# A hybrid mLSTM / GLA / sparse-attention block: x in its own pool, background work in smaller portions, high parts first

## The chip, the cores and the metric

The kernel runs on one core of a Trainium2 chip. The metric is the time of one execution in device microseconds (us): the median of three runs of the kernel before is 1209.51 us (1208.49 to 1209.81). The profile is of one more execution.

## What is computed

Two layers (`DEPTH = 2`) work on x, 512 rows by 1024 columns in float32. Each layer normalises x, multiplies it by a wide weight matrix (9312 columns), runs three mixers on the pieces, and multiplies the gated results back to 1024 columns:

```python
p = split_columns(rmsnorm(x, norm_g) @ w_in)
...
hm = mlstm_chunkwise(heads(mq, ML_HEADS), heads(mk, ML_HEADS), heads(p['ml_v'], ML_HEADS), li, lf).astype(dt)
...
hg = gla_chunked(heads(p['gla_q'], GLA_HEADS), heads(p['gla_k'], GLA_HEADS),
                 heads(p['gla_v'], GLA_HEADS), heads(la, GLA_HEADS)).astype(dt)
...
hd = dsa_sparse_attention(dq, dk, heads(p['dsa_v'], DSA_HEADS), iq, p['idx_k'], iw, rel_bias, topk)
...
y = jnp.concatenate([y_ml, y_gla, y_dsa], axis=-1) @ w_out
return x + y
```

The sparse attention picks 128 keys for each query by an index score; the kernel finds them with 16 rounds of "eight largest, then strike them out".

## The kernel before

**Three passes for a product.** A float32 product is made of three fast passes. Each operand is split in a high part (a copy in the type `F32R`, on ACT) and a low part (the rest, on DVE). `mm3` issues high times high, high times low and low times high into one PSUM sum. The high and low parts of the normalised, transposed x are `xhi` and `xlo`, 8 slices of 128 rows by 512 columns each. Weights arrive in pieces of 128 x 1024 (`raw`), which `prepare()` turns into `hi` (ACT) and `lo` (DVE), one piece ahead of the need. `need(p)` makes sure that both parts of a piece are issued.

**The three kinds of projection.** `wide` has x as the stationary operand and the weights moving (PSUM tile `pn`, 512 columns); a unit has four pieces and four blocks `sb` of 128 rows, and a block takes 24 matmuls, 6 of each piece. `proj_t` has the weights stationary and x moving (`pt`, 512 columns, or 384 for the index queries). `w_out_part` has the gated results `yhi`, `ylo` stationary and the weights moving (`pw`, 512 columns). Twelve `wide` units stand in a layer. All matmul, copy and DMA calls go through one recorder, so that nearly all rows of the trace have the line L178; the tiles' names tell the place.

**Background work.** Everything else (the mLSTM products `psS` and `pom`, GLA's `psga`, `psst`, `pog`, the index scores `pss`, the attention `psl`, `pst`, `pod`, the transposes `psx`, `psy`, `psq`) is written as generators. After every few projection matmuls the program calls `tick()`, which lets `Background` run steps of those tasks that a clock model says are ready. The model is only a planner: it runs while the program is built and sets the order in which instructions are issued; on the chip each engine goes through its queue in that order and waits on semaphores. `TICK_PE = 1.3` is how much TensorE time, in the model's us, the steps of one tick may add before it ends; `PRIORITY` sorts the ready tasks, low numbers first (`"scores": 0`, `"gla": 2`, `"sel": 4`). The model books 512 columns of a projection at 512/2210 + 0.002 = 0.2337 us (`Meter.cost`).

**Where tiles lie.** SBUF pools lie one behind the other in each partition in the order of their creation: `const`, `par`, `wp`, `wk`. Tiles with tags of their own follow each other in the order of first use, sizes rounded up to 32 bytes. `xhi` and `xlo` (16384 bytes a partition each) and `qz0`, `qz1` (2048 each) stand at the end of `const`, with `lev` (256) behind them; then `par` has two `pv` (448 each) and `zw` (1024). Then come the 12 weight tiles of `wp` (4096 each, tag `w`), and right behind them in `wk` the ten tiles with tag `t4` (4096 each), among them `yhi`, `ylo` and mLSTM's `ml_q`, `ml_k`. From the start of `xhi` to that of the first weight tile it is 2 x 16384 + 2 x 2048 + 256 + 2 x 448 + 1024 = 39040 bytes, which is 76 x 512 + 128. All slices of x, of the weights and of `t4` tiles that matmuls take begin at multiples of 512 bytes from their tile's start.

The leading block of a `wide` unit goes through the same path as the others, piece by piece:

```python
for j in range(2):
    k = 2 * i + j
    mm3(pss[sb], xhi[:, k, s], xlo[:, k, s], wh[j], wl[j], k == 0, k == KT - 1)
```

Of the kernel before, what the change touches and what calls it, by code (L numbers as in the profile page):

```python
# [10 lines left out]
F32 = mybir.dt.float32  # L11
F32R = mybir.dt.float32r
# [8 lines left out]
S = 512  # L21
D = 1024
DEPTH = 2
NB = S // 128
KT = D // 128
# [104 lines left out]


PAR_W = 108
TICK_PE = 1.3
TICK_K, TICK_T = 4, 2
SEMAPHORE, PIPE = 0.2, 0.13
BEHIND = {"sel": ("dve",)}
BACKLOG = {None: 11.0, "sel": 0.3}
ALONE = ("gla", "ml", "sel", "scores")
BUFFERS = {"gla": 6, "dsa": 4, "ml": 4, "mlv": 1, "conv": 2, "qk": 2, "y": 2, "scores": 4, "gates": 5}
PRIORITY = {"conv": 1, "y": -1, "norm": 0, "split": 0, "ml": 0, "mlv": 2, "scores": 0, "gla": 2, "dsa": 2, "sel": 4}  # L140


def pack_parameters(p):
# [131 lines left out]
class Background:  # L275
# [41 lines left out]
    def pick(self):  # L317
        for task in sorted(self.tasks, key=lambda t: PRIORITY.get(t["kind"], 1)):
            if self.startable(task) and self.due(task) <= self.clock.at["pe"]:
                return task  # L320

    def tick(self):
        end = self.clock.at["pe"] + TICK_PE
        task = self.pick()
        while task and self.clock.at["pe"] < end:
            self.step(task)
            task = self.pick()
# [14 lines left out]
def hybrid_kernel(ctx, tc, a, out, dbg=None):  # L342
    bass_nc = tc.nc
    clock = Clock()
# [14 lines left out]
    W_BUFS, RAWS, LOAD = 12, 2, 4.5  # L359
    const = ctx.enter_context(tc.tile_pool(name="const", bufs=1))  # L360
    par = ctx.enter_context(tc.tile_pool(name="par", bufs=2))
    wp = ctx.enter_context(tc.tile_pool(name="wp", bufs=2))
    wk = ctx.enter_context(tc.tile_pool(name="wk", bufs=2))
    sm = ctx.enter_context(tc.tile_pool(name="sm", bufs=8))
# [4 lines left out]
    def pp(name):  # L369
        t = psp.tile([128, 512], F32, tag="pp", name=name)  # L370
        clock.ring("pp", t, 3)
        return t
# [37 lines left out]
        nc.vector.memset(head[r, odd:odd + 1], 1.0)  # L410
    pad = const.tile([128, 8], F32, name="pad")
    nc.vector.memset(pad, 0.0)
    xhi = const.tile([128, KT, S], F32R, name="xhi")
    xlo = const.tile([128, KT, S], F32R, name="xlo")
    qzs = [const.tile([128, 2, 64 * NB], F32, name=f"qz{i}") for i in range(2)]
    for t in qzs:
        for odd, r in enumerate(HALVES):
            nc.gpsimd.memset(t[r, 1 - odd], 0.0)
# [45 lines left out]
    to_split, half_done, held, wanted = [], [], [], []  # L464
    state = {"used": 0, "raw": 0, "unit": 0}

    def w_tile(name, dtype):
        return wp.tile([128, 1024], dtype, tag="w", name=name, bufs=W_BUFS)

    def make_room(most=RAWS):  # L470
        while to_load and state["raw"] < most:
            if state["used"] + 1 > W_BUFS - (2 if any(p.hi is None for p in wanted) or not held else 0):
                break
            p = to_load.pop(0)
            state["used"] += 1
            state["raw"] += 1
            p.raw = w_tile("raw", F32)
            nc.sync.dma_start(p.raw, a["w_pack"][p.layer, p.at])
            p.loaded = clock.at["pe"] + LOAD
            to_split.append(p)  # L480

    def prepare():
        if half_done:
            p = half_done.pop()
            lo = w_tile("lo", F32R)
            nc.vector.tensor_sub(lo, p.raw, p.hi.bitcast(F32))
            state["used"] -= 1
            state["raw"] -= 1
            p.parts = [[t[:, c:c + p.n] for c in range(0, 1024, p.n)] for t in (p.hi, lo)]
            make_room()  # L490
        if to_split and to_split[0].loaded <= clock.at["pe"] and state["used"] + 2 <= W_BUFS:
            p = to_split.pop(0)
            state["used"] += 2
            p.hi = w_tile("hi", F32R)
            nc.scalar.activation(p.hi, p.raw, AF.Copy)
            half_done.append(p)

    def need(p):
        while p.parts is None:
            if not half_done:  # L500
                clock.at["pe"] = max(clock.at["pe"], to_split[0].loaded)
            prepare()
        return p.parts

    def take(kind, at=None):
        spec, pieces = units[state["unit"]]
        assert spec[0] == kind and (at is None or spec[1] == at), (spec, kind, at)
        state["unit"] += 1
        wanted.extend(pieces)
        held.extend(pieces)  # L510
        return pieces


    def give_back():
        p = held.pop(0)
        wanted.remove(p)
        state["used"] -= 2
        make_room()
# [3 lines left out]
    def tick():  # L522
        prepare()
        bg.tick()

    def mm3(ps, lh, ll, rh, rl, first, last):
        nc.tensor.matmul(ps, lhsT=lh, rhs=rh, start=first, stop=False)
        nc.tensor.matmul(ps, lhsT=lh, rhs=rl, start=False, stop=False)
        nc.tensor.matmul(ps, lhsT=ll, rhs=rh, start=False, stop=last)


    def proj_t(pieces, blk, s0=0, last=False):
        ps = pp("pt")
        c = slice(128 * blk, 128 * blk + 128)
        for k in range(KT):
            n = KT // len(pieces)
            wh, wl = need(pieces[k // n])
            mm3(ps[:, s0:S], wh[k % n][:, c], wl[k % n][:, c], xhi[:, k, s0:S], xlo[:, k, s0:S], k == 0, k == KT - 1)
            if last and k % n == n - 1:
                give_back()  # L540
            if k % TICK_T == TICK_T - 1 and k < KT - 1:
                tick()
        return ps
# [3 lines left out]
    def wide(pieces, f, before=None):  # L547
        pss = {}

        def part(sb, i):  # L550
            if i == 0:
                if before:
                    before(sb)
                pss[sb] = pp("pn")
            s = slice(128 * sb, 128 * sb + 128)
            wh, wl = need(pieces[i])
# [3 lines that stand above are left out]
            if sb == NB - 1:  # L560
                give_back()
            if i == 3:
                f(sb, pss.pop(sb))
            tick()

        lone = NB if before else NB - 2
        for sb in range(lone):
            for i in range(4):
                part(sb, i)
        if not before:  # L570
            for i in range(4):
                for sb in range(lone, NB):
                    part(sb, i)
# [104 lines left out]
    for layer in range(DEPTH):  # L678
# [45 lines left out]
        def y_group(name, hns, g0=0):  # L724
            yt, tasks = [], []

            def part(sb, ps):
                tasks.append(bg.start(y_part(yt, hns, ps, sb), "y"))
            wide(take("wide", OFF[name] + 256 * g0), part)
            return yt, tasks  # L730

        def w_out_part(q, yt, tasks, after=None):
            pieces = take("out", 512 * q)

            pss = {}
# [465 lines left out]
        zw = par.tile([80, 256], F32R, name="zw", bufs=1)  # L1201
        t_zw = bg.add(rank_weights())
        wide(take("wide", OFF["gla_v"]), keep_gv, lambda sb: bg.drain(norms[sb]))
        norms.clear()
        if layer == 0:
# [3 lines left out]
        ps = proj_t(w, 0, 0, True)  # L1209
# [47 lines left out]
        def dsa_qk_unit(g):  # L1257
            dst = [blocks(t4("dqk"), 2) for _ in range(2)]
            t_qk = []

            def part(sb, ps):
                t_qk.append(bg.start(qk_part(dst, ps, sb), "qk"))
            wide(take("wide", OFF["dsa_q"] + 256 * g), part)
            qks.append((dst, t_qk))
            if vs:
                dsa_tasks(g)
# [67 lines left out]
        for n, step in enumerate(PLAN):  # L1334
# [3 lines left out]
            _, name, g0, quarter = step  # L1338
# [32 lines left out]
```

## Time and profile before

| | |
|---|---|
| median of three runs | 1209.51 us (1208.49 to 1209.81) |
| the profiled execution | 1210.23 us, its span 1208.5 us |
| TensorE: matmuls busy | 1190.5 us, 99% of the span, 6004 of them |
| VectorE (DVE) busy | 832.7 us, 69% |
| ScalarE (ACT) busy | 600.4 us, 50% |
| GpSimd (POOL) busy | 169.6 us, 14% |
| DMA | 107.70 MB, mean 89 GB/s |
| granted TensorE clock, mean | 0.999 |

A page of the profile gives each engine's busy time, the idle time with what ended it, and the chain of work that ended last. PE is TensorE's matmuls, PEld its weight loads. Matmuls overlap in their pipeline, so the duration of one says little: what a matmul costs is the distance to the start of the next, which the chain's pieces show (so many matmuls in so many us).

### The profile page before, as it was taken

The numbers are of one execution on the slowest core, as the hardware profiler recorded it, in microseconds if no ns is written. First come the engines' busy times: TensorE is split into PE (matmuls) and PEld (weight loads), VectorE is DVE, ScalarE is ACT, GpSimd is POOL, SyncE is SP. The second block draws the span as 40 slices with busy tenths as digits, with TensorE's granted clock in tenths as the row PEclk, the third lists the DMA queues.
The fourth block names the chain that finished last, engine by engine and source line by source line (L and its number), as shares of the span: only waits on it lengthen the run. The fifth ranks groups of instructions, "written<-read, shape, count | busy, mean of one in ns | idle before, by whom it ended". The sixth has DMA issues, their size and how long they took to land.

```text
span 1208.5 us, 16501 instructions
## 1 busy us (share of the span) xinstructions
PE 1190.5 (99%) x6004; PEld 970.7 (80%) x6004; DVE 832.7 (69%) x1651; ACT 600.4 (50%) x1334; POOL 169.6 (14%) x309
## 2 busy tenths in 40 slices
PE   6999999999999999999999999999999999999998
PEld 4877788888888887888888778888888888887887
DVE  5577887977777766365566888878777778554643
ACT  6565546554353354762366654564453443646421
POOL 2101212320100011120010023041210010123000
PEclk9999999999999999999999999999999999999999
DMA  5333121221322233132224222222222223233221
GB/s 198 109 99 106 62 88 62 88 80 53 105 97 70 77 116 131 63 106 85 70 71 140 65 75 93 82 71 79 71 71 87 96 71 105 71 105 123 70 86 71
DMA packets 35152, 107.70 MB, mean 89 GB/s; under 512 B 5028, under 2 KB 8388, under 8 KB 35072
## 3 DMA queue, kind: packets, MB, share of 16 engines
q1 hardware_dynamic: 33136, 104.89, 26.7%
q0 software_dynamic: 1200, 1.36, 0.3%
q8 instruction: 47, 0.77, 0.3%
q10 hardware_dynamic: 736, 0.41, 0.1%
q14 instruction: 33, 0.27, 0.1%
HBM read 104.48 MB, written 3.43 MB: 89 GB/s over the span
## 4 chain that ended last, share of the span: by engine, by line
PE 88%; DVE 1%; issue 0%; ACT 0%; ACTq 0%
PE pn L178 42%; PE pt L178 17%; PE pw L178 14%; PE psS L178 3%; PE pom L178 2%; PE psga L178 1%; PE pod L178 1%; PE psl L178 1%; PE pog L178 1%; PE psy L178 1%; PE pst L178 1%; PE pss L178 1%; PE psq L178 1%; PE psx L178 0%; PE psst L178 0%; PE psd L178 0%
## 5 line engine op out<-in xcount | busy, mean ns | idle before, releaser
L178 DVE TENSOR_TENSOR lo<-raw,hi 128x1024 fp32r<-128x1024 f32 x178 | 219.4, 1233 | 141.1 <-ACT hi L178 134.5
L178 PE MATMUL pn<-hi,xhi 128*128 128x512 f32 x768 | 312.9, 407 | 0.0
L178 PE MATMUL pn<-lo,xhi 128*128 128x512 f32 x768 | 303.8, 396 | 0.6 <-DVE lo L178 0.6
L178 PE MATMUL pn<-hi,xlo 128*128 128x512 f32 x768 | 304.0, 396 | 0.0
L178 ACT ACTIVATE hi<-raw 128x1024 fp32r<-128x1024 f32 x178 | 188.7, 1060 | 202.4 <-PE pn L178 90.3
L178 PEld LDWEIGHTS pn<-hi,xlo 128*128 128x128 f32 x768 | 144.8, 189 | 35.2 <-DVE xlo L178 1.2
L178 PEld LDWEIGHTS pn<-lo,xhi 128*128 128x128 f32 x768 | 145.2, 189 | 32.2 <-DVE lo L178 1.2
L178 PEld LDWEIGHTS pn<-hi,xhi 128*128 128x128 f32 x768 | 145.2, 189 | 31.9 <-issue 0.8
L178 PE MATMUL pt<-xhi,hi 128*128 128x512 f32 (+1 forms) x400 | 158.7, 397 | 0.0
L178 PE MATMUL pt<-xhi,lo 128*128 128x512 f32 (+1 forms) x400 | 154.3, 386 | 0.0
L178 PE MATMUL pt<-xlo,hi 128*128 128x512 f32 (+1 forms) x400 | 154.2, 385 | 0.0
L178 PE MATMUL pw<-hi,yhi 128*128 128x512 f32 x256 | 101.7, 397 | 0.0
L178 PE MATMUL pw<-hi,ylo 128*128 128x512 f32 x256 | 99.9, 390 | 0.0
L178 PE MATMUL pw<-lo,yhi 128*128 128x512 f32 x256 | 99.7, 390 | 0.0
L178 PEld LDWEIGHTS pt<-xhi,hi 128*128 128x128 f32 x400 | 75.2, 188 | 17.6 <-issue 3.8
L178 PEld LDWEIGHTS pt<-xhi,lo 128*128 128x128 f32 x400 | 75.2, 188 | 14.9
L178 DVE TENSOR_TENSOR xr<-pw,xr 128x512 f32<-128x512 f32 x64 | 44.1, 689 | 60.6 <-PE pw L178 60.5
L178 PEld LDWEIGHTS pt<-xlo,hi 128*128 128x128 f32 x400 | 75.3, 188 | 12.6
L178 DVE SCALAR_TENSOR_TENSOR cacc<-cbuf,pv,cacc 128x512 f32<-128x512 f32 x96 | 73.3, 764 | 2.5 <-ACT el L178 0.2
L178 PEld LDWEIGHTS pw<-hi,ylo 128*128 128x128 f32 x256 | 48.0, 188 | 10.2
L178 PEld LDWEIGHTS pw<-lo,yhi 128*128 128x128 f32 x256 | 48.1, 188 | 9.3
L178 PEld LDWEIGHTS pw<-hi,yhi 128*128 128x128 f32 x256 | 48.1, 188 | 9.3
(188 smaller groups left out, 1661.3 us busy)
## 6 DMA issues: line engine op xcount, KB each, us to landing
raw<-w_pack SPq DMA_DIRECT2D x178, 512.0 KB, 3.5
xr<-x SPq DMA_DIRECT2D x4, 512.0 KB, 7.6
negm<-negm SPq DMA_DIRECT2D x8, 256.0 KB, 3.7
bs<-skew SPq DMA_DIRECT2D x8, 256.0 KB, 4.0
out_dram<-xr SPq DMA_DIRECT2D x8, 256.0 KB, 2.0
bs<-skew SPq DMA_DIRECT2D x8, 192.0 KB, 4.4
skew<-flat POOLq DMA_DIRECT2D x1, 1280.0 KB, 15.9
bs<-skew SPq DMA_DIRECT2D x8, 128.0 KB, 4.6
```

The lines of the kernel that those rows point to most:

```text
L178: return f(*args, **kw)
```

## The change

Three things are edited. `xhi`, `xlo`, `qz0` and `qz1` move from `const` to a pool `xt`, made between `par` and `wp`. From the start of `xhi` to the first weight tile it is now 2 x 16384 + 2 x 2048 = 36864 bytes, which is 72 x 512. `TICK_PE` goes from 1.3 to 0.7, and the priority of `scores` from 0 to 3, behind `gla`. And the leading block of each `wide` unit gets a function of its own, `first()`: for all four pieces the two passes that need only `hi`, then for all four the pass that needs `lo`; it ticks after each piece of the first half and after every other piece of the second.

```diff
-TICK_PE = 1.3
+TICK_PE = 0.7
...
-PRIORITY = {"conv": 1, "y": -1, "norm": 0, "split": 0, "ml": 0, "mlv": 2, "scores": 0, "gla": 2, "dsa": 2, "sel": 4}
+PRIORITY = {"conv": 1, "y": -1, "norm": 0, "split": 0, "ml": 0, "mlv": 2, "scores": 3, "gla": 2, "dsa": 2, "sel": 4}
...
+    xt = ctx.enter_context(tc.tile_pool(name="xt", bufs=1))
...
-    xhi = const.tile([128, KT, S], F32R, name="xhi")
-    xlo = const.tile([128, KT, S], F32R, name="xlo")
-    qzs = [const.tile([128, 2, 64 * NB], F32, name=f"qz{i}") for i in range(2)]
+    xhi = xt.tile([128, KT, S], F32R, name="xhi")
+    xlo = xt.tile([128, KT, S], F32R, name="xlo")
+    qzs = [xt.tile([128, 2, 64 * NB], F32, name=f"qz{i}") for i in range(2)]
...
+    def need_high(p):
+        while p.hi is None:
+            if not half_done:
+                clock.at["pe"] = max(clock.at["pe"], to_split[0].loaded)
+            prepare()
+        return [p.hi[:, c:c + p.n] for c in range(0, 1024, p.n)]
...
+        def first():
+            if before:
+                before(0)
+            ps = pp("pn")
+            s = slice(0, 128)
+            for i in range(4):
+                wh = need_high(pieces[i])
+                for j in range(2):
+                    k = 2 * i + j
+                    nc.tensor.matmul(ps, lhsT=xhi[:, k, s], rhs=wh[j], start=k == 0, stop=False)
+                    nc.tensor.matmul(ps, lhsT=xlo[:, k, s], rhs=wh[j], start=False, stop=False)
+                tick()
+            for i in range(4):
+                wl = need(pieces[i])[1]
+                for j in range(2):
+                    k = 2 * i + j
+                    nc.tensor.matmul(ps, lhsT=xhi[:, k, s], rhs=wl[j], start=False, stop=k == KT - 1)
+                if i % 2 == 0:
+                    tick()
+            f(0, ps)
+            tick()
...
         lone = NB if before else NB - 2
-        for sb in range(lone):
+        first()
+        for sb in range(1, lone):
             for i in range(4):
                 part(sb, i)
```

The order of issue shows three places. The first is PE in the first layer's first `wide` unit, right at the start (`psx` are transposes of x, `pn` the projection; numbers tell buffers apart, `hi_165` and `lo_190` are the parts of the fourth piece). The end of the leading block before:

```order
L178 MATMUL pn_183<-lo_190,xhi_100 128x512
L178 MATMUL pn_183<-hi_165,xlo_101 128x512
L178 MATMUL psx_237<-ident_82,xs_176 128x128 x4
L178 MATMUL psx_246<-ident_82,xs_176 128x128 x4
L178 MATMUL psx_260<-ident_82,xs_208 128x128 x4
L178 MATMUL pn_273<-hi_128,xhi_100 128x512
```

Now (the fourth piece is `hi_168`, `lo_191`):

```order
L178 MATMUL pn_186<-hi_168,xhi_103 128x512
L178 MATMUL pn_186<-hi_168,xlo_104 128x512
L178 MATMUL pn_186<-lo_134,xhi_103 128x512 x2
L178 MATMUL pn_186<-lo_147,xhi_103 128x512 x2
L178 MATMUL pn_186<-lo_164,xhi_103 128x512 x2
L178 MATMUL pn_186<-lo_191,xhi_103 128x512 x2
L178 MATMUL psx_238<-ident_85,xs_179 128x128 x4
L178 MATMUL psx_247<-ident_85,xs_179 128x128 x4
L178 MATMUL pn_266<-hi_131,xhi_103 128x512
```

The eight products with `lo` stand behind the sixteen with `hi`; and behind them 8 transposes where 12 stood, since block 2's (`xs_208`) moved back.

The second place is ACT at the same time: `zw` belongs to GLA's weights, `gv` empties the projection's PSUM tile, `xs` scales x for the transposes of blocks 1 to 3, `xhi` empties these.

```order
 L178 ACTIVATE zw<-wa 16x256 x2
+L178 ACTIVATE xs<-xr,rx 128x1024
 L178 ACTIVATE gv<-pn 128x256 x2
-L178 ACTIVATE xs<-xr,rx 128x1024 x2
-L178 ACTIVATE xhi<-psx,pv 128x128 x8
 L178 ACTIVATE xs<-xr,rx 128x1024
 L178 ACTIVATE xhi<-psx,pv 128x128 x16
-L178 ACTIVATE gv<-pn 128x256 x4
+L178 ACTIVATE xs<-xr,rx 128x1024
```

Block 1's `xs` is now ahead of `gv`, and block 2's `xs` behind it.

The third place is PE in the first mLSTM unit, where GLA's products (`psga`) and mLSTM's (`psS`) stand between the projection's matmuls. Before:

```order
L178 MATMUL psS<-ml_q,ml_k 128x384 x6
L178 MATMUL psga<-qz_102,dec 64x2x32 x8
L178 MATMUL pn<-hi,xhi 128x512
L178 MATMUL pn<-lo,xhi 128x512
L178 MATMUL pn<-hi,xlo 128x512
```

Now, behind the same `psS` row and three more `pn` rows like the first three of these:

```order
L178 MATMUL pn<-hi,xhi 128x512
L178 MATMUL pn<-lo,xhi 128x512
L178 MATMUL pn<-hi,xlo 128x512
L178 MATMUL psga<-qz_105,dec 64x2x32 x8
L178 MATMUL pn<-hi,xhi 128x512
```

What one tick issued together is now spread over two, with six projection matmuls between. Over the whole program the order has 4080 projection matmuls in both kernels; background work cuts them into 201 stretches before and 221 now. Of the 3312 matmuls of 512 columns that have x as an operand (`pn`, `pt`), the order now has 526 in stretches of up to 6, 560 in stretches of 8 to 12, 560 in stretches of 13 to 24, and 1666 in longer ones.

## Rows read from the trace of the kernel before

**Rows 1.** The page: busy time by engine, share of the span, instructions; then PE's clock.

```profile
PE 1190.5 (99%) x6004; PEld 970.7 (80%) x6004; DVE 832.7 (69%) x1651; ACT 600.4 (50%) x1334; POOL 169.6 (14%) x309
...
PEclk9999999999999999999999999999999999999999
```

**Rows 2.** Waits of PE over the whole span: total us, times, longest.

```profile
PE psx L178 <- ACT xs L178: 11.9, 2, 8.4
PE psga L178 <- DVE qz L178: 1.1, 1, 1.1
PE psst L178 <- ACT kdn L178: 0.7, 1, 0.7
PE pn L178 <- DVE lo L178: 0.6, 1, 0.6
```

**Rows 3.** The chain that ended last, long stretches: start us, us, what.

```profile
328.39 22.39 PE pt L178 x96
350.79 14.00 PE pn L178 x60
...
1019.43 16.74 PE pn L178 x72
...
1185.77 19.07 PE pw L178 x84
```

**Rows 4.** The same chain, short stretches.

```profile
368.63 2.79 PE pn L178 x12
...
403.75 2.77 PE pw L178 x12
406.52 0.44 PE psy L178 x4
406.96 1.39 PE pw L178 x6
...
386.42 1.40 PE pn L178 x6
...
191.28 4.19 PE pn L178 x18
...
605.37 4.13 PE pw L178 x18
```

**Rows 5.** PE in order of time: mLSTM products of 512 columns between projection matmuls.

```profile
142.49 1.53 PE L178 MATMUL psS<-ml_q,ml_k 128*128 128x512 f32 x6
...
261.11 1.56 PE L178 MATMUL psS<-ml_q,ml_k 128*128 128x512 f32 x6
```

**Rows 6.** The chain around GLA's products in the first layer.

```profile
146.49 0.62 PE psga L178 x16
147.11 1.59 PE pn L178 x6
```

**Rows 7.** Busy us by stretch: width, PE, PEld, DVE, ACT, POOL, PE's clock, DMA share, GB/s.

```profile
120.00:140.00 20.00, 18.32 (x99) 14.23 (x98) 17.78 (x27) 10.46 (x18) 4.87 (x12) 1.00 0.23 75
140.00:160.00 20.00, 20.00 (x133) 16.13 (x132) 18.74 (x35) 11.06 (x21) 7.24 (x15) 1.00 0.27 80
700.00:720.00 20.00, 19.35 (x100) 15.28 (x101) 16.80 (x29) 11.36 (x23) 4.47 (x9) 1.00 0.16 54
```

**Rows 8.** ACT at the start, in order of time.

```profile
17.48 0.85 ACT L178 ACTIVATE zw<-wa 16x256 fp32r<-16x256 f32 x2 [0.72 <-DMA wa<-gla_w_a]
18.35 0.66 ACT L178 ACTIVATE gv<-pn 128x256 f32<-128x256 f32 x2
19.03 2.19 ACT L178 ACTIVATE xs<-xr,rx 128x1024 f32<-128x1024 f32 x2
21.13 2.15 ACT L178 ACTIVATE xhi<-psx,pv 128x128 fp32r<-128x128 f32 x8
```

**Rows 9.** PE at the start, in order of time.

```profile
20.24 1.74 PE L178 MATMUL psx<-ident,xs 128*128 128x128 f32 x12 [3.57 <-ACT xs L178]
21.69 0.71 PE L178 MATMUL pn<-hi,xhi 128*128 128x512 f32 x1
```

## The prediction

> **What bounds the kernel now.** I read the page first: PE is busy 99% of the span at the full clock, no other engine over 69% [rows 1]. Then the waits of PE: 14.3 us in all, of which 11.9 are two waits on `xs` at the start [rows 2]. So from 21 us on time is what PE's own instructions take, end to end, and the chain that ended last gives their price: a piece "x72" of 16.74 us is 72 matmuls, 232.5 ns from one start to the next. The reader should then compare pieces that do the same work. All are 128 x 128 by 512 columns, three passes, yet the long projection pieces with x (`pn`, `pt`) run at 14.00/60 = 233.3, 16.74/72 = 232.5 and 22.39/96 = 233.2 ns, the output projection (`pw`) at 19.07/84 = 227.0 [rows 3]. Short pieces don't differ: six take 1.40 with `pn`, 1.39 with `pw`; twelve 2.79 and 2.77; eighteen 4.19 and 4.13 [rows 4]. The faster pace is something that a stretch settles into.
>
> What sets `pn` and `pt` apart from `pw` can't be which operand moves: in `pn` it is the weights, in `pt` x, and both are slow; `pw` has the weights moving, as `pn`. It is not the neighbours either, since the pace holds over 96 matmuls. What remains is where x lies: its start is 76 x 512 + 128 bytes in front of the weights', while `yhi`, `ylo` and the weights are whole multiples of 512 apart. A third product has both operands in `t4` tiles, so also whole multiples: `psS`. Its first batch of six takes 1.53 us; less the last one's 0.39 that is 5 steps of 228 ns, in the middle of slow `pn` [rows 5]. Another takes 1.56, 234 ns, so this is support and no proof: six are too few to settle.
>
> **The change part by part.**
>
> *x in its own pool.* Now x, too, lies a whole multiple of 512 bytes (72) in front of the weights. I take the pace of `pw` for `pn` and `pt`, by length of stretch. Up to 6: 526 matmuls at (1.40 - 1.39)/6 = 1.7 ns, 0.9 us. 8 to 12: 560 at (2.79 - 2.77)/12 = 1.7, 0.9 us. 13 to 24: 560 at (4.19 - 4.13)/18 = 3.3, 1.9 us. Longer: 1666 at 232.9 (mean of the two `pn` rows) less 227.0 = 5.9, 9.8 us [rows 3, 4]. The sum is 13.5 us. Bounds: nothing, if the start is not the cause; 3312 x 5.9 = 19.5 us, if stretches settle at once. I keep the middle, since the short `pw` rows are the nearest. The 192 matmuls of 384 columns I cost at nothing.
>
> Here the Trainium skill speaks against the change: SBUF — State Buffer gives TensorE a second, independent read port for weight loads (section "A bandwidth-pool intuition that's wrong (but worth ruling out)"), and asks of an operand's start no more than a multiple of its element size, as legality, not speed ("Operand start alignment"). By it the two paces could not come from the start of x; the pool would be worth 0 and the sum +0.8 us instead of -11.2. The rows show two paces, so I go by them.
>
> *Smaller portions, `scores` behind `gla`.* No work is added: PE has the same instructions, DMA the same transfers; on SP's queue `bs` and `raw` change places at a few points, on POOL's (14% busy [rows 1]) GLA's differences move ahead of `acc`. The first layer's last selection goes back by some 40 projection matmuls in the order, and the attention task that needs it goes back with it, so nobody waits for it longer on the chip. What grows is the number of stretches, 201 to 221. A cut by transposes costs nothing beyond these: six `pw` right behind four `psy` (0.44) take 1.39, and the 1.40 of six `pn` is the pace of a long stretch [rows 3, 4]. A cut by GLA's products costs: the six `pn` behind `psga` take 1.59, 0.19 more [rows 6]. Of the 20 new cuts I count 3 more returns from such float32 products in the order, 0.6 us; bounds 0 and 20 x 0.19 = 3.8 us.
>
> *High ahead of low.* Each leading block (24 of them) keeps its 24 matmuls; the `lo` of its third piece is wanted 8 matmuls, about 1.9 us, later. The one wait on `lo` is 0.6 us [rows 2], in the stretch 120 to 140 us, where DVE is busy 17.8 of 20 us and PE idles 1.7 [rows 7]. DVE owes `psga` its operand right after, and the wait there (1.1) would grow by what the other loses. I cost this at 0; bounds -0.6 and 0. In a faster kernel these dense stretches give something back: with DVE at 17.8 and 18.7 of 20 us between 120 and 160 [rows 7], PE can't arrive earlier than DVE lets it. PE gains about 1.5 us on the way to 160 us (160/1210 of the sum); the second layer has such a stretch too (700 to 720: DVE 16.8, PE idle 0.65 [rows 7]), so up to 3 us come back as waits on DVE. I take half, +1.5.
>
> *The start.* The leading block doesn't end sooner: it waits for `xlo` as before and is followed by the wait on `xs`. ACT now issues `xs` right behind `zw`, at 18.35 instead of 19.03, so the transposes begin at about 19.55 instead of 20.24 [rows 8, 9]. But `gv` (0.66) and block 2's `xs` (1.1, half of 2.19) then stand ahead of `xhi`: 18.35 + 1.1 + 0.66 + 1.1 = 21.2, against 21.13 [rows 8]. The first `pn` behind them moves by +0.1, and four transposes (0.44, as `psy`) that filled the idle time come later. In exchange `xhi` of block 2 is no longer behind block 3's `xs`. I take +0.2; bounds -0.7 and +0.6.
>
> *Sum:* -13.5 + 0.6 + 0 + 1.5 + 0.2 = -11.2 us, from the profiled execution's 1210.23: 1199.0. The median of the runs is 0.7 us below that execution, so 1198.3 as a median.
>
> **The rivals.**
>
> *The waits take it back.* The planner books 233.7 ns a projection matmul. If the chip does it in 227, PE reaches every place that waits on ACT or DVE earlier than booked. For it: DVE's 90% and the waits on `qz`, `kdn` and `lo` [rows 2, 7]. Against it: outside these stretches DVE and ACT have room (69% and 50% [rows 1]) and waits in all the rest of the kernel are 2.4 us [rows 2]. If half of the pool's gain comes back, 6.7 us instead of 1.5, it is 1203.5.
>
> *The pool does nothing.* The pace stays at 233 because it comes from something else that `pw` has. The second `psS` row, at 234 [rows 5], speaks for it; that `pn` and `pt` share one pace with opposite roles speaks against. Then the sum is +0.6 + 0.2, with no more waits: 1210.3. This is where the skill's rule of independent ports would end (SBUF — State Buffer); the traces so far bear it out only in short stretches.
>
> *Slower: the cuts.* The place is every return from a background portion; the price is the 0.19 us behind `psga` [rows 6], at each of the 20 new ones, 3.8 us; it makes the kernel slower when the pool gives less than 1.4 us, since 2.4 us are the 0.2% that a measurement can tell from no change. With the pool at nothing: 1209.5 + 3.8 + 0.2 = 1213.5. Against it: the other rows of short stretches show no price.
>
> **How the numbers follow.** My forecast, the pace of `pw` for x with little returned, 0.80: 1192 to 1202. The waits take half, 0.07: 1202 to 1207. The pool does nothing, 0.08: 1207 to 1212. The cuts, 0.05: above 1212. The forecast's low end is the pool's 19.5 with 1.5 returned, rounded in by a little; the range reaches from there into the second case, 1192 to 1204, some 0.83. Faster by over 0.2% is the first two cases, 0.87; within 0.2% the third, 0.08; slower 0.05. The likeliest case's time is 1198.3.
>
> **What would show it.** Right: long pieces of `pn` and `pt` in the chain at 227 ns a matmul, the pieces of six and twelve as before; PE's waits behind 30 us between 2 and 5 us, on DVE, between 110 and 180 us and 590 us later; the first wait on `xs` unchanged at 8.4, the second some 0.7 us shorter; `pn` behind `psga` still at 1.59. Wrong: `pn` at 233 with x moved, which strikes the largest term; or `pn` at 227 with the sum of PE's waits above 7 us, which means that the planner's order, not PE's pace, sets the end.

## The result and the profile after

The median of four runs is 1194.05 us (1193.87 to 1196.43), against 1209.34 for four runs of the kernel before: a ratio of 0.9879, 95% interval 0.9862 to 0.9896. That is 15.3 us less, against 11.2 predicted, and inside the range. The profiled execution is the slowest of the four, 1196.43 us with a span of 1194.7; why, stands in the last section.

The page's busy times and PE's clock, to lay beside [rows 1]:

```profile
PE 1176.7 (98%) x6004; PEld 969.4 (81%) x6004; DVE 834.4 (70%) x1651; ACT 600.0 (50%) x1334; POOL 173.4 (15%) x309
...
PEclk9999999999999999999999999999999999999999
```

PE has the same 6004 matmuls and is busy 13.8 us less; no other engine's work changed by more than 4 us. So the time did not come out of waits. PE's waits are, over the whole span (us in total, times, longest), to lay beside [rows 2]:

```profile
PE psx L178 <- ACT xs L178: 9.6, 2, 8.3
PE psga L178 <- DVE qz L178: 3.5, 4, 1.7
PE pn L178 <- ACT xhi L178: 0.7, 1, 0.7
PE pn L178 <- DVE xlo L178: 0.3, 1, 0.3
```

Together 14.1 us, where it was 14.3: the second wait on `xs` is shorter, and GLA's `psga` waits more on its operand `qz`. What became cheaper is the matmul itself. The chain that ended last (start us, us, what) has these long pieces:

```profile
895.60 16.35 PE pw L178 x72
911.95 21.76 PE pt L178 x96
933.71 16.32 PE pn L178 x72
...
1171.76 19.07 PE pw L178 x84
```

96 `pt` take 21.76 us, 226.7 ns each, where [rows 3] had 22.39; 72 `pn` take 16.32, also 226.7, for 16.74; `pw` is at 227 as it was. The two paces have become one. Short pieces of the same chain:

```profile
1073.46 1.39 PE pn L178 x6
...
1079.61 2.75 PE pn L178 x12
...
1075.07 4.10 PE pn L178 x18
...
866.26 1.59 PE pn L178 x6
```

Six are where they were, twelve 0.04 and eighteen 0.09 us shorter than in [rows 4]; the last row is six `pn` behind `psga`, at the 1.59 of [rows 6].

In the stretches where I had put the new waits, and in two others (columns as in [rows 7]):

```profile
120.00:140.00 20.00, 20.00 (x125) 15.90 (x125) 16.16 (x26) 10.13 (x19) 6.34 (x13) 1.00 0.22 67
140.00:160.00 20.00, 20.00 (x129) 16.43 (x126) 16.21 (x30) 9.62 (x19) 4.05 (x10) 1.00 0.33 106
160.00:180.00 20.00, 19.85 (x125) 16.52 (x124) 15.95 (x32) 12.50 (x36) 1.94 (x3) 1.00 0.17 53
245.00:265.00 20.00, 18.27 (x89) 14.83 (x88) 14.15 (x23) 8.06 (x15) 4.78 (x10) 0.91 0.18 66
740.00:760.00 20.00, 19.84 (x128) 16.11 (x127) 19.09 (x39) 9.25 (x17) 0.96 (x5) 1.00 0.25 79
840.00:860.00 20.00, 18.59 (x115) 15.19 (x113) 16.56 (x29) 11.07 (x21) 5.87 (x10) 1.00 0.25 79
```

Between 120 and 160 us DVE has 1.6 and 2.5 us less to do than before, and PE doesn't idle there any more. The four waits on `qz` come at 161, 254.9, 749 and 842 us. The first and third, where I expected them, are short: PE idles 0.15 and 0.16 us in their stretches. The other two, outside, make up the rest, 1.7 and 1.4, though DVE is busy only 14.15 and 16.56 of 20 us around them (13.12 and 13.60 in the same stretches before, where PE did not idle): an average over 20 us doesn't show a moment in which one operand is late.

The start. ACT and PE in order of time, to lay beside [rows 8, 9]:

```profile
16.96 0.85 ACT L178 ACTIVATE zw<-wa 16x256 fp32r<-16x256 f32 x2 [0.72 <-DMA wa<-gla_w_a]
17.96 1.15 ACT L178 ACTIVATE xs<-xr,rx 128x1024 f32<-128x1024 f32 x1
19.02 0.64 ACT L178 ACTIVATE gv<-pn 128x256 f32<-128x256 f32 x2
19.55 1.15 ACT L178 ACTIVATE xs<-xr,rx 128x1024 f32<-128x1024 f32 x1
20.59 2.17 ACT L178 ACTIVATE xhi<-psx,pv 128x128 fp32r<-128x128 f32 x8
```

```profile
19.17 1.09 PE L178 MATMUL psx<-ident,xs 128*128 128x128 f32 x8 [1.29 <-ACT xs L178]
21.00 0.80 PE L178 MATMUL pn<-hi,xhi 128*128 128x512 f32 x1 [0.74 <-ACT xhi L178]
```

`xs` stands right behind `zw`, and `gv` and the second `xs` ahead of `xhi`, as the order said. `psx` comes 1.07 us earlier, 0.69 expected: `zw`, which waits for the DMA of `wa`, was itself half a microsecond earlier in this execution. The second wait on `xs` is 1.29 us where it was 3.57, so 2.3 shorter where I had expected 0.7. Of this 1.07 is the earlier `psx`. The other 1.2 us are no gain: the leading block ended that much later, because PE started only 10 matmuls between 10 and 14 us, where it started 16 before (columns as in [rows 7]; first the kernel before, then the change):

```profile
10.00:14.00 4.00, 4.00 (x16) 2.89 (x15) 3.82 (x12) 4.00 (x10) 0.00 (x0) 1.00 1.03 415
...
10.00:14.00 4.00, 3.66 (x10) 2.57 (x9) 3.82 (x12) 4.00 (x10) 0.00 (x0) 1.00 1.03 412
```

For part of this time the matmuls start 0.43 us apart, the pace of the stretches with a low clock in the last section; but both lines have a clock of 1.00, so the cause is not shown.

### The profile page after: what moved, and what is told of

Same layout as the page of the kernel before. It is cut to its first block, busy times and chain, and to the rows that moved or that the text cites. A ratio compares the mean times of both kernels' runs of the same rounds, so it can differ in the third digit from the quotient of the medians.

```text
span 1194.7 us, 16479 instructions
## 1 busy us (share of the span) xinstructions
PE 1176.7 (98%) x6004; PEld 969.4 (81%) x6004; DVE 834.4 (70%) x1651; ACT 600.0 (50%) x1334; POOL 173.4 (15%) x309
## 5 line engine op out<-in xcount | busy, mean ns | idle before, releaser
L178 PE MATMUL pn<-lo,xhi 128*128 128x512 f32 x768 | 276.1, 394 | 0.0
L178 PEld LDWEIGHTS pt<-xhi,lo 128*128 128x128 f32 x400 | 75.1, 188 | 13.8
L178 POOL TENSOR_TENSOR dec<-ta 128x256 f32<-128x256 f32 x56 | 54.4, 990 | 14.8 <-PE psd L178 8.3
```

Of the source, the lines that this page charges most:

```text
L178: return f(*args, **kw)
```

## The experiments

Three theories were open. **Places:** matmuls are faster because of how far the two operands lie apart. **Order:** smaller portions and high-ahead-of-low have a share in the 15 us. **Pool:** x got faster by having a pool of its own, or an absolute place. Four versions, each run several times, divide the change. Those that look for the rule were run once each, with a profiled clock of 0.999 or 1.000 but for one, named below.

### The pool alone

The kernel before, with `xhi`, `xlo`, `qz0`, `qz1` in `xt` and nothing else:

```diff
+    xt = ctx.enter_context(tc.tile_pool(name="xt", bufs=1))
-    xhi = const.tile([128, KT, S], F32R, name="xhi")
+    xhi = xt.tile([128, KT, S], F32R, name="xhi")
```

(`xlo` and the two `qz` likewise.)

> The kernel before with nothing changed but the pool of x. Theory (the distance from x to the weights, modulo 512 bytes, sets the pace): long pieces of pn and pt run at 227 ns a matmul as in the changed kernel, and the time is 1192 to 1197 us, nearly the whole gain. Rival (the order, smaller portions and high parts first, made the gain): the time stays within 2.4 us of the kernel before.

Measured: 1194.53 us (1193.61 to 1196.24), ratio 0.9878 (0.9865 to 0.9892). This is the whole gain, and the long pieces have the new pace:

```profile
910.95 21.76 PE pt L178 x96
932.71 16.32 PE pn L178 x72
```

Its program has PE's matmuls in the same order as the kernel before, so the two traces can be compared one matmul at a time: the distance from each start to the next, behind 33 us, without the two steps that hold a wait. For the 512 columns with x, by length of stretch between two pieces of background work, the differences add up to: up to six, -0.82 us (462 matmuls); 7 to 12, -1.32 (480); 13 to 24, -2.26 (576); longer, -9.79 (1732). `pt` of 384 columns gives -0.36, the mLSTM products `psS` and `pom` -0.39, `pw` -0.06; with the small rest it is -15.1 in all.

### The order alone

The change, with x back in `const` (remainder 128 of the distance by 512, as before):

```diff
-    xhi = xt.tile([128, KT, S], F32R, name="xhi")
+    xhi = const.tile([128, KT, S], F32R, name="xhi")
```

> The changed kernel with x back in its old place. Theory: long pieces of pn and pt at 232.5 to 233.3 ns again, pw at 227, and the time within 2.4 us of the kernel before (1207 to 1212). Rival (the order made the gain): 1194 to 1198 us.

Measured: 1208.02 us (1207.75 to 1210.94), ratio 0.9992 (0.9983 to 1.0001): no difference from the kernel before that can be told. Its long pieces are those of the kernel before:

```profile
919.89 22.39 PE pt L178 x96
...
1018.04 16.74 PE pn L178 x72
```

### The two halves of the order

The change without `first()` (`no_first`), the leading block going through `part` as before:

```diff
-        first()
-        for sb in range(1, lone):
+        for sb in range(lone):
```

> The changed kernel with the leading block in its old order, piece by piece. Theory (the leading block's order is worth nothing): within 2.4 us of the changed kernel's 1194.05. Rival: 2 to 4 us slower, since waits on the low part of the weights come back (0.6 us before) and the start is later.

And the change with the old portions:

```diff
-TICK_PE = 0.7
+TICK_PE = 1.3
...
-... "scores": 3, ...
+... "scores": 0, ...
```

> The changed kernel with portions of 1.3 and scores first, as before. Theory (my sum priced smaller portions at +0.6 us, for more returns from GLA's products): 0 to 1 us faster than the changed kernel, within 2.4 us of it. Rival: smaller portions saved waits on DVE, and this one is 1 to 4 us slower, with more than 3.5 us of waits of PE behind 30 us.

Measured: without `first()` 1193.05 us (1192.52 to 1193.27), ratio 0.9864 (0.985 to 0.9877); with the old portions 1194.1 (1193.37 to 1195.0), ratio 0.9873 (0.986 to 0.9887). Portions are worth nothing that can be told. `first()` gains nothing and may cost up to 1 us; the runs don't overlap with those of the change, but 1 us is less than what I said can be told, and the single runs below with the same order of issue (remainder 256 and both shifts) have 1193.65 to 1194.28. The wait on `qz` points the same way. Without `first()`, all waits of PE behind 30 us are:

```profile
PE psga L178 <- DVE qz L178: 2.2, 4, 1.0
```

In the change it is 3.5, and 3.1 to 3.6 in those three runs. The wait on `lo`, 0.6 before and 0.8 with the pool alone, did not come back without `first()`, though the rival had said it would; nor is it among PE's waits with the old portions. So either edit removes it by itself. With high parts ahead, DVE's `lo` of a whole block is wanted in one go; that this is what delays `qz` was only argued.

### Other distances from x to the weights

The change, with something between the `qz` tiles and the weights. First 64 bytes (`rest_64`):

```diff
+    gap = xt.tile([128, 16], F32, name="gap")
+    nc.gpsimd.memset(gap[:, 0:1], 0.0)
```

> The changed kernel with 64 empty bytes between x and the weights, so a distance of 72 x 512 + 64. Theory (only a rest of 0 settles): long pieces of pn and pt at 230 to 234 ns, pw at 227, time 1205 to 1212. Rival 1 (only the place of x in SBUF counts, not its distance): 227 ns and 1193 to 1197 us. Rival 2 (the pattern repeats every 64 bytes): 227 ns as well, but then rests of 128 would have been fast too, and they were not.

Measured: 1202.53 us, half of the gain lost, which is less than my theory's 1205 to 1212. Its long pieces:

```profile
916.09 22.40 PE pt L178 x96
938.49 16.80 PE pn L178 x72
...
1013.89 16.48 PE pn L178 x72
```

`pt` is at 233.3 ns, `pn` at 233.3 in one stretch and 228.9 in the other, below the 230 that I had given. Over the whole trace most long `pn` stretches settle at 229; the two that follow a `pt` x96 directly have 233.3, so what went before seems to have a say. Second, 256 bytes: `lev` (256 bytes) in `xt` instead of `const`.

```diff
-    lev = const.tile([128, 8, 32], U8, name="lev")[:, 0:len(LEVELS)]
+    lev = xt.tile([128, 8, 32], U8, name="lev")[:, 0:len(LEVELS)]
```

> The changed kernel with the tile lev (256 bytes) between x and the weights, a distance of 72 x 512 + 256. Theory: not at 227 but at 230 to 234 ns in long pieces, time 1205 to 1212. Rival (the pattern repeats every 256 bytes): 227 ns, 1193 to 1197 us. A pace below 227 would show that a rest of 0 isn't the best one.

Measured: 1193.65 us, as fast as the change. Here my theory fell in the form in which I held it, "whole multiples of 512":

```profile
909.11 21.76 PE pt L178 x96
930.87 16.32 PE pn L178 x72
```

So the distance counts by 256 bytes, as far as two fast remainders (0 and 256 by 512) can show it. Third, 1920 bytes, which is remainder 384 by 512 and 128 by 256: the pool `par` made behind `xt` instead of ahead of it.

```diff
-    par = ctx.enter_context(tc.tile_pool(name="par", bufs=2))
...
     xt = ctx.enter_context(tc.tile_pool(name="xt", bufs=1))
+    par = ctx.enter_context(tc.tile_pool(name="par", bufs=2))
```

> The changed kernel with the pool par between x and the weights, a distance of 75 x 512 + 384. Theory: as a rest of 128 with the sides exchanged, 230 to 234 ns in long pieces, time 1205 to 1212. Rival (it is that x lies in a pool of its own): 227 ns, 1193 to 1197 us.

Measured: 1207.94 us, with 22.39 for 96 `pt` and 16.80 for 72 `pn`, as before the change; and x still has a pool of its own, so the pool as such does nothing. Last, the smallest gap, 32 bytes (`gap` with 8 columns instead of 16):

> The smallest gap that the allocation allows: 32 bytes between x and the weights, remainder 32 by 256. If only whole multiples of 256 are good: pn and pt slower than 226.7 ns in long stretches, as in rest_64 or nearer to it, 1198 to 1203 us. Rival, the two operands only have to lie within some tens of bytes of the multiple (a row of 64 bytes, say, is read as one): 226.7 ns and 1194 us.

Measured: 1210.39 us, outside my 1198 to 1203, worse than 64 bytes and no better than the kernel before. Its mean clock was 0.997; the profiled execution of the change, with the same clock, was 2.4 us above its others, so some 2 us of the time may be that (an estimate). The pace itself leaves no doubt: this near miss of the multiple is worth nothing:

```profile
922.03 22.40 PE pt L178 x96
944.44 16.80 PE pn L178 x72
...
1185.71 19.08 PE pw L178 x84
```

### The absolute place

The change with everything moved and the distance kept. By 256 bytes down, `lev` going behind all of it:

```diff
-    lev = const.tile([128, 8, 32], U8, name="lev")[:, 0:len(LEVELS)]
+    lev = sm.tile([128, 8, 32], U8, tag="lev", name="lev", bufs=1)[:, 0:len(LEVELS)]
```

> The changed kernel with the tile lev moved behind everything, so that x, the weights and the t4 tiles all lie 256 bytes lower, with the same distances. Theory (distance): 227 ns in long pieces of pn, pt and pw, 1193 to 1197 us. Rival (the start of x itself counts, 384 modulo 512 in the changed kernel, 128 here): the pace of pn and pt, perhaps of pw too, goes to 230 ns and more.

Measured: 1194.28 us, unchanged. With a period of 256 this proves little, so a shift of 64 bytes followed, the `gap` of 64 bytes put in front of `xhi`:

> x, the weights and the t4 tiles all begin 64 bytes further on; the distance from x to the weights stays 36864 bytes, remainder 0 by 256. If only the distance between the two operands counts: pn, pt and pw in long stretches at 226.7 ns a matmul, 1194 us. Rival, the place of an operand by itself counts: pn and pt as in rest_64 (229 and 233 ns), pw slower too, 1202 us or more.

Measured: 1193.71 us, unchanged, with x, the weights and `t4` 64 bytes off the multiples on which they lay:

```profile
909.29 21.76 PE pt L178 x96
931.05 16.32 PE pn L178 x72
...
1169.04 19.07 PE pw L178 x84
```

So of these two it is the distance of the two operands that counts, and not the place.

### The other product made slow

The change with a 64-byte pool between `wp` and `wk`. Now `yhi` and `ylo` are 64 bytes off, and x is not:

```diff
+    gp = ctx.enter_context(tc.tile_pool(name="gp", bufs=1))
     wk = ctx.enter_context(tc.tile_pool(name="wk", bufs=2))
...
+    gap = gp.tile([128, 16], F32, name="gap")
+    nc.gpsimd.memset(gap[:, 0:1], 0.0)
```

> x and the weights as in the change; the t4 tiles, with yhi and ylo, lie 64 bytes further from the weights. If the distance of the two operands counts, whichever they are, the output projection, fast in every run so far, gets slow: pw moves the weights with yhi standing, so the moving operand begins 64 bytes earlier by 256 than the standing one, the sign that pt had in rest_64, where it took 233.3 ns a matmul. So pw in long stretches at 233 ns (19.6 us for 84 instead of 19.07), pn and pt at 226.7; some 700 steps by 4 to 6.6 ns, +3 to +4.5 us, about 1198 us. If only who moves counts (the weights, as in pn of rest_64): pw at 229 to 230, +1 to +2 us. Rival, only x has the effect (its own buffers or its way of being written): pw at 226.7, 1194 us.

Measured: 1198.36 us, 4.3 more than the change. `pw`, at 227 ns in every other run, is slow, and `pn` and `pt` stay fast:

```profile
912.17 21.77 PE pt L178 x96
933.94 16.32 PE pn L178 x72
...
1173.13 19.62 PE pw L178 x84
```

84 `pw` at 233.6 ns, where they took 19.07 us. So the effect belongs to no one tensor and to no way of writing it.

### What is left in the order

Without `first()`, and with the planner booking the pace that the chip now has:

```diff
-                return max(n, 256) / 2210 + 0.002
+                return 0.2267 if n == 512 else max(n, 256) / 2210 + 0.002
```

> The change without the new function for the leading block, and the planner books 0.2267 us for a projection matmul of 512 columns instead of 0.2337, the pace that the chip now has. If the order of issue does not bound the kernel: waits of PE behind 30 us stay at 1 to 3.5 us and the time at 1193.0 us, as in no_first, give or take 1. Rival, the planner's old price makes PE arrive too early everywhere: the waits on qz go to below 1 us and the time to 1191 us or less.

Measured: 1193.43 us (1192.87 to 1193.65), ratio 0.9861 (0.9843 to 0.9879); the same as without `first()` alone. The waits on `qz` are gone, as the rival said, but another has come instead, and the rival's 1191 us did not:

```profile
PE pskd L178 <- DVE za L178: 1.5, 1, 1.5
```

No version tried beats "the change without `first()`" (1193.05), which beats both kernels, the changed one by an amount at the edge of what can be told.

## Why the prediction was right, and where not

The sum was 4.1 us short of the 15.3 measured: the mechanism of its largest term was right, and sizes were off.

*The pool, -13.5: right in kind, 1.6 too small.* Measured alone, -15.1 by the medians (1194.53 against 1209.59), with what it gives back in waits already in it. The trace of that run has other counts of matmuls than my terms, so I compare the gain of one matmul: stretches up to six 1.7 ns expected, 1.8 found; 8 to 12, 1.7 and 2.7; 13 to 24, 3.3 and 3.9; longer, 5.9 and 5.7. With my counts that makes 0.9, 1.5, 2.2 and 9.4 us. The term that was most off is that of 8 to 12. I took 1.7 ns from one `pw` piece of twelve at 2.77; the same chain has six more, at 2.73 to 2.76, so it was the slowest of its kind. For eighteen it was so too: I took 4.13, and the chain has two more, both at 4.09. The other shortfall is what I costed at nothing: 384 columns gave 0.36, and about 0.5 came from products that I had not thought of, `psS` and `pom` most of it.

*Why x counts: right, with the wrong number.* "x is not a whole multiple of 512 from the weights" holds only because 128 is no multiple of 256. With 256 in place of 512 the forecast would have been the same, and a kernel with a remainder of 256 would have been called slow, wrongly. The argument by elimination (neither the moving operand nor the neighbours) was borne out by the run that made `pw` slow. My support from `psS` was not: over the kernel before its 48 products of 512 columns start 231.5 ns apart on the mean, no fast pace, and with the pool alone 226.7, though neither of their operands moved (all that lies behind `xt` begins where it did). So these short batches between slow `pn` were slow as well, at a distance that is good by the rule; why, no run shows, and the rule below is one for long stretches.

The rows show paces that follow the distance of the two operands, at the three absolute places that were tried. The Trainium skill, SBUF — State Buffer, gives weight loads a second, independent read port (section "A bandwidth-pool intuition that's wrong (but worth ruling out)"), by which nothing should have moved. Here page and measurement differ, 226.7 against 233.3 ns, and the measurement decides; what happens inside, no run shows.

*Smaller portions, +0.6: nothing found.* 1194.1 against 1194.05. What the counted returns from float32 products cost is less than can be told; `psga`'s neighbours kept their price of 1.59.

*High ahead of low, 0: 0 to +1.* The bound of my term ended at 0 on the costly side, and the medians put it at 1194.05 - 1193.05 = +1.0; if that holds, the bound was drawn too tight. I argued that `psga`'s wait would grow by what the one on `lo` loses. With the old portions that is what came: against the pool alone `lo` loses its 0.8 and `qz` goes from 1.2 to 1.9. With the new ones `lo` has nothing left to lose, and `qz` still goes from 2.2 to 3.5; that I had not thought of.

*Given back, +1.5: near in size, but not by my account.* Waits of PE behind 30 us are 3.5 us, inside "2 to 5", and were 2.4. They are on DVE, but 0.3 of them lie in the expected stretches and 3.1 outside. My account was that a faster PE runs into DVE's dense stretches; the pool alone, which has that pace and the old order, gives back 0.3 (2.7 us of waits). The two long waits come from the new order: with x back in its old place, at the slow pace, they stand at the same two products, at 256.7 and 849.8 us, and are PE's only waits behind 30 us:

```profile
PE psga L178 <- DVE qz L178: 2.1, 2, 1.1
```

From there to the change the waits grow by 1.4, but to the change without `first()` by 0.1 only; so it is in part luck that the total came near my 1.5. The run whose planner books the new pace has 1.5 us of waits, and no gain from it. In the times, the new order makes -1.3 to -1.6 at the old place of x (1208.02 against 1209.34 and 1209.59), where I had +0.8; this is less than can be told. The pool on top of it makes -14.0 (to 1194.05), where the sum had -13.5 + 1.5 = -12.0.

*The start, +0.2: not measured,* since the low clock in the last section hides it. `psx` came 1.07 earlier, and not 0.69, and the first `pn` behind it at 21.00 where it was 21.69, of which `zw` makes 0.52 each time. The sign that the second wait on `xs` would be 0.7 shorter did not come as said, see the result.

The rivals: waits that take half back didn't come (3.5 us in all). The pool that does nothing is refuted by its run alone, and the cuts by theirs.

## What to carry to other kernels

Where two kinds of matmul of one shape run at two paces in long stretches, compare the distances of their operands in SBUF before looking for waits: here 512 columns cost 226.7 ns when the stationary and the moving operand begin a whole multiple of 256 bytes apart, and 229 to 234 ns at remainders 32, 64 and 128. Other remainders, and operands of another type, were not tried. Here the pace was worth 15 us, and all waits of PE behind 30 us were 2.4; so lay out pools by the pace, small tiles behind the large ones or padded to the multiple. And test each part of a bundle by itself: of three edits one carried everything, and one may have cost.

## What the runs showed that was not expected

*A near miss can cost as much as a far one.* With the weights behind x by 36864 bytes plus 0, 32, 64, 256 and 1920: 1194.05 (median), 1210.39, 1202.53, 1193.65 and 1207.94 us. The sign seems to matter too: where the moving operand begins 64 bytes late (`pn`), the pace wavers between 229 and 233 ns; where it begins 64 early it is 233.3 (`pt`, x moving) and 233.6 (`pw` in the run that made it slow, weights moving).

*The clock after a wait.* The profiled execution of the change was 2.3 to 2.6 us above the others of its kind. Two stretches with a lower granted clock (0.5 is 1.2 GHz, 1.0 is 2.4) show where most of it went; columns as in [rows 7]:

```profile
20.00:22.00 2.00, 1.26 (x5) 0.52 (x3) 0.24 (x1) 2.00 (x7) 0.41 (x1) 0.69 0.23 94
22.00:24.00 2.00, 2.00 (x5) 1.39 (x5) 1.92 (x8) 0.76 (x3) 0.00 (x0) 0.50 0.00 0
...
256.00:258.00 2.00, 2.00 (x7) 1.57 (x6) 1.96 (x6) 0.54 (x1) 0.00 (x0) 0.57 0.00 0
258.00:260.00 2.00, 2.00 (x7) 1.52 (x6) 1.96 (x3) 0.51 (x1) 0.00 (x0) 0.57 0.00 0
260.00:262.00 2.00, 2.00 (x10) 1.67 (x9) 0.01 (x1) 0.69 (x1) 0.00 (x0) 1.00 0.33 63
```

The second follows the 1.7 us wait on `qz`: PE starts 7 matmuls in 2 us, where some 9 go at full clock (about 1 us lost in each of the two, an estimate from these counts). The first follows the waits on `xs` and `xhi`. The run with remainder 256 has the change's order of issue, and there the same place went at full clock, with 13 matmuls for 5:

```profile
22.00:24.00 2.00, 1.83 (x13) 1.60 (x13) 1.93 (x8) 0.92 (x4) 0.00 (x0) 1.00 0.00 0
```

At the second place the run with everything 256 bytes lower, again of the same order, waits 1.8 us on `qz` and keeps 1.00, with 10 matmuls in each of the next 2 us. So after like waits the clock fell in one execution and not in another; what decides it, no run shows. The kernel before had such a stretch at the start of its profiled execution too (0.50 between 22 and 24 us), so the start can't be compared between single profiles to better than about 1 us.
